# Moving transposed blocks through DRAM: two reads over all 128 partitions in place of four over 32

## The chip, the core and the metric

The kernel runs on one core of a Trainium2 chip. The metric is device time in microseconds (us), the median of several executions of the whole program; less is better. The core has five engines that work side by side: TensorE (PE, matrix products), VectorE (DVE), ScalarE (ACT), GpSimd (POOL) and SyncE (SP). Here SP computes nothing: it issues nearly all DMA transfers, one after another. A DMA is carried out by 16 DMA engines; each of them takes its part of the transfers of one queue in the order in which they were issued.

## What is computed

The input x is 512 tokens of width 1024, in float32. Two layers follow each other, each one normalisation, one input projection, an attention, a gate and an output projection that is added to x:

```
hn   = rms_norm(x, gain)
proj = hn @ w_in                 # queries, keys, values, gate
q, k = rms_norm per head of 64   # 16 heads
out  = softmax(q.k * scale + bias) @ v
x    = x + (out * silu(gate)) @ w_out
```

Layer 0 has three dilation groups (1, 4 and 16) with sliding windows, each with q, k and v of its own, merged by their softmax denominators. Layer 1 is a neighbourhood attention on a grid of 8 x 64 tokens. Products are made from float32 values split into a high and a low part, three matmuls for one product.

## The kernel before

**Tiling.** The 16 heads are worked off in pairs, `hc` = 0 to 7 (`NHC`), 128 columns at a time. For each pair `main_a` (layer 0) or `main_b` (layer 1) projects q, k, v and the gate on PE. In the same stream of PE instructions stands the attention of the pair before, which the generator `side` places between them: PE's order is written out by hand, by a clock in the program (`clock`, `later_on`, `tick`) that counts nominal matmul time. `later_on(delay, job)` issues a DMA when that clock has come far enough; the order of SP's queue follows from it, and SP takes it strictly in order. A DMA that has to wait holds everything behind it on SP.

**Weights.** `raws` (L175) loads blocks of up to 512 KB into three buffers `wraw`. `split` makes the high part `wh` on ACT (L127) and the low part `wl` on POOL or DVE (L131), four buffers each; PE uses them in the projections (`acc`). A load into a `wraw` buffer waits until the block that was there has been split.

**Bias.** `bias_a` loads six small tables for the next pair, `e0` and `e12` (L687 and L692, 704 KB together), from `l_d` in DRAM. The source of each is a pattern of 4 x 32 rows, and its destination has 128 partitions:

```
bass.AP(l0_d.tensor, l0_d.offset + h * 1600 + 127, [[400, 4], [-4, 32], [1, 256]])
```

**The two moves.** A transpose of a 128 x 512 block is made on VectorE in 32 x 32 squares (`nc.vector.transpose`) and completed by a trip through DRAM which takes the squares to other partitions.

- `move_q` (L568) does this for the projected q and k of layer 0, for the pairs 0 and 2 to 5 (`moved`). VectorE transposes the squares of `rawq` (`turn_q`); four writes (L576) put `rawq` into `qd`, write `a` the a-th quarter of every partition's row, 2 KB for each of 128 partitions; four reads (L583) bring `qd` into `qt`. Read `a` fills the 32 partitions from 32a, with four runs of 2 KB each, and needs write `a` alone. From `qt`, `split_q` makes k0h (L602), q0h (L621), k0l and q0l, and with these PE makes the scores (`log`). All four parts must be there.
- `turner` (L713) does it for the softmax probabilities `p`. `put` transposes into `tr` (L724). `send` writes `tr` to `td` (L733) and reads `td` into `pt` (L737), again four and four. In layer 0 each pair from 0 to 6 sends two blocks (u = 0 and 1) of 512 columns a part, in layer 1 each pair from 0 to 5 one of 448. From `pt` PE multiplies the probabilities with v (`o`) during the next pair.

The writes are issued 700 (q) or 1200 to 1500 (p) nominal nanoseconds apart, and the reads 6800 or 9500 to 12000 after the writes. On SP the order in a pair of layer 0 is: four td writes, a weight load, a pt read, six bias loads, a weight load, the remaining pt reads, td writes of the second block with a weight load between, pt reads with weight loads between, four qd writes, a weight load, and the qt reads, also with a weight load between.

Of the kernel before, what the change touches and what calls it, by code (L numbers as in the profile page):

```python
# [13 lines left out]
F32 = mybir.dt.float32  # L14
# [8 lines left out]
P = 128  # L23
# [19 lines left out]
def tile_hybrid_encoder(  # L43
# [13 lines left out]
    nc = tc.nc  # L57
# [8 lines left out]
    dr = ctx.enter_context(tc.tile_pool(name="dr", bufs=1, space=DRAM))  # L66
# [159 lines left out]
    def later_on(delay, job):  # L226

        timers.append((clock[0] + delay, job))
        timers.sort(key=lambda t: t[0])
# [305 lines left out]
    def q_tiles():  # L535


        return (
            wk.tile([P, 512], F32R, tag="q0h", name="q0h", bufs=1),
            wk.tile([P, 512], F32R, tag="q0l", name="q0l", bufs=1),  # L540
            wk.tile([P, 4, 4, P], F32, tag="q12", name="qt", bufs=1),
            wk.tile([P, EXT], F32R, tag="k0h", name="k0h", bufs=1),
            wk.tile([P, EXT], F32R, tag="k0l", name="k0l", bufs=1),
        )

    def q_a(hc):

        yield "wait", ("rawq", hc), 15000 if hc < NHC - 2 else 13000
        raw = st.pop(("rawq", hc))
        if moved(hc):  # L550
            move_q(hc, raw)
            return
        st["q", hc] = q0h, q0l, qt, k0h, k0l = q_tiles()

        tp = transpose4(raw, 0)
        nc.scalar.copy(tjr(q0h), to_tjr(tp))
        nc.vector.tensor_sub(tjr(q0l), to_tjr(tp), tjr(q0h.bitcast(F32)))
        yield
        tp = transpose4(raw, 3 * P)
        put_k([(trj(k0h[:, 64:EXT]), trj(k0l[:, 64:EXT]), to_trj(tp))], 0)  # L560
        yield
        for g in range(2):
            tp = transpose4(raw, (g + 1) * P)
            nc.vector.tensor_copy(qt[:, :, 1 + g, :].rearrange("p t (j r) -> p t j r", j=4), to_tjr(tp))
            yield
        stamp["q", hc] = 0

    def move_q(hc, raw):  # L568

        d = dr.tile([4, P, 512], F32, name="qd", tag="qd", bufs=2)  # L570
        tiles = q_tiles()
        qt, left = tiles[2], [4]

        def write(a):
            src = raw[:, 4 * a : 4 * a + 4].rearrange("p f i r -> p (f i r)")
            tc.keep_in_program_order(nc.sync.dma_start(d[a], src))  # L576
            if a == 3:
                stamp["q", hc] = 0

        def read(a):  # L580
            dst = qt[32 * a : 32 * a + 32].rearrange("k t f x -> k t (f x)")
            src = d[a].rearrange("(t k) x -> k t x", t=4)
            tc.keep_in_program_order(nc.sync.dma_start(dst, src))  # L583
            left[0] -= 1

        for a in range(4):
            later_on(700 * a, partial(write, a))
            later_on(6800 + 700 * a, partial(read, a))

        def land():  # L590
            yield "wait", ("rawq", hc), 27000
            assert not left[0]
            split_q(*tiles)
            st["q", hc] = tiles
            yield

        st["land", hc] = land()

    def split_q(q0h, q0l, qt, k0h, k0l):
        src = qt[:, :, 3, :].rearrange("p t (j r) -> p t r j", j=4)  # L600
        trj4 = lambda t: t[:, 64:EXT].rearrange("p (t r j) -> p t r j", t=4, j=4)
        nc.scalar.copy(trj4(k0h), src)  # L602
        by_t = lambda t: t.rearrange("p (t x) -> p t x", t=4)
        put_k([(by_t(q0h), by_t(q0l), qt[:, :, 0, :])], 0)
        nc.vector.tensor_sub(trj4(k0l), src, trj4(k0h.bitcast(F32)))
# [107 lines left out]
    class turner:  # L713
# [1 line left out]


        def __init__(self, run):
            self.run, self.left = run, 4
            self.t = wk.tile([P, 2048], F32, tag="tr", name="tr", bufs=1)

        def put(self, src, n, off):
# [4 lines left out]
        def send(self, dst, wait, pace):  # L726

            run = self.run
            d = dr.tile([4, P, run], F32, tag="td", name="td", bufs=2)
            place = dst.rearrange("p (a x) -> p a x", a=4)  # L730

            def write(b):
                tc.keep_in_program_order(nc.sync.dma_start(d[b], self.t[:, b * run : b * run + run]))  # L733

            def read(b):
                src = d[b].rearrange("(a k) x -> k a x", a=4)
                tc.keep_in_program_order(nc.sync.dma_start(place[32 * b : 32 * b + 32], src))  # L737
                self.left -= 1

            for b in range(4):  # L740
                later_on(pace * b, partial(write, b))
                later_on(wait + pace * b, partial(read, b))

    def attn_a(hc):
        e0, e12 = st.pop(("e", hc))
# [538 lines left out]
```

## Time and profile before

| | |
|---|---|
| median of 3 executions | 888.09 us (885.46 to 892.52) |
| the profiled execution | 889.36 us |
| its span, first to last instruction | 887.5 us |
| mean granted TensorE clock | 0.983 |
| PE, PE weight load busy | 853.6, 710.0 us |
| DVE, ACT, POOL busy | 513.6, 431.8, 297.8 us |
| moved by DMA | 139.15 MB, mean 157 GB/s |

The page gives busy time by engine, the chain of work that ended last (followed back from the last instruction to what released it) and the DMA issues by size. "A <- B" in the table of waits says that A's engine sat idle until B was done, with the total in us, the count and the longest. In a timeline, a row is start, duration, engine, line, operation, output <- input and count. In a table of windows, the columns are the stretch, its length, busy time (and count) of PE, PE weight load, DVE, ACT and POOL, the granted TensorE clock, the mean busy share of the 16 DMA engines, and GB/s. The chain's rows are start, duration and what ran. SPq is SP's queue: the duration there is that of the issue and not that of the transfer.

### The profile page before, as it was taken

How to read it: one execution, taken by the hardware profiler on the slowest of the kernel's cores; microseconds unless marked ns; L12 is line 12 of the kernel's file. 1: busy time of each engine (PE TensorE's matmuls, PEld its weight loads, DVE VectorE, ACT ScalarE, POOL GpSimd, SP SyncE). 2: the span in 40 equal slices, each digit the busy share in tenths (PEclk: the TensorE clock that was granted, in tenths of full speed). 3: DMA queues.
4: the chain of work that ended last, by engine and by line, in shares of the span. 5: the costliest groups of instructions: out<-in, count | busy, mean ns of one | idle time of the engine just before them, and what ended most of it. 6: DMA issues, size and time to landing. Idle time of an engine off the chain costs nothing.

```text
span 887.5 us, 15473 instructions
## 1 busy us (share of the span) xinstructions
PE 853.6 (96%) x5563; PEld 710.0 (80%) x5563; DVE 513.6 (58%) x1333; ACT 431.8 (49%) x924; POOL 297.8 (34%) x493
## 2 busy tenths in 40 slices
PE   9999999997999799699799999999999999999998
PEld 7787778785788588578678788788989988889786
DVE  7363585672664566367267584537565666666743
ACT  7533565432552552354264454446465556665541
POOL 2342431441442342144143144111433445433411
PEclk9999999999899899799899999999999999999999
DMA  6356366568359268448738366146226556466323
GB/s 240 111 152 193 119 178 169 174 198 198 108 164 256 84 173 245 83 140 229 186 116 220 102 179 182 56 157 200 96 89 167 164 154 174 136 166 185 101 94 129
DMA packets 65469, 139.15 MB, mean 157 GB/s; under 512 B 7024, under 2 KB 24368, under 8 KB 65392
## 3 DMA queue, kind: packets, MB, share of 16 engines
q1 hardware_dynamic: 65104, 138.15, 54.7%
q8 instruction: 44, 0.72, 0.4%
q14 instruction: 33, 0.27, 0.1%
q10 hardware_dynamic: 288, 0.01, 0.0%
HBM read 108.06 MB, written 30.07 MB: 156 GB/s over the span
## 4 chain that ended last, share of the span: by engine, by line
PE 86%; DMA 6%; ACT 3%; DVE 2%; POOL 1%; issue 1%; SPq 1%; ACTq 0%; POOLq 0%; DVEq 0%
PE acc L206 72%; DMA qt<-qd 5%; PE log L206 5%; PE o L206 5%; PE tp L210 3%; ACT wh L127 1%; POOL wl L131 1%; DMA pt<-td 1%; ACT p L1073 1%; ACT k0h L602 0%; DMA hg<-in_head_gain 0%; ACT rawk L458 0%; DVE hn_l L378 0%; DVE q0l L623 0%; ACT p L652 0%
## 5 line engine op out<-in xcount | busy, mean ns | idle before, releaser
L127 ACT CAST wh<-wraw 128x512 fp32r<-128x512 f32 (+1 forms) x276 | 161.7, 587 | 290.4 <-PE acc L206 251.1
L206 PE MATMUL acc<-wh,hn_h 128*128 128x512 f32 (+1 forms) x768 | 294.7, 384 | 1.7 <-ACT rawk L458 1.1
L206 PE MATMUL acc<-wl,hn_h 128*128 128x512 f32 (+1 forms) x768 | 286.1, 373 | 0.7 <-DVE wl L131 0.7
L206 PE MATMUL acc<-wh,hn_l 128*128 128x512 f32 (+1 forms) x768 | 286.1, 373 | 0.0
L131 POOL TENSOR_TENSOR wl<-wraw,wh 128x512 fp32r<-128x512 f32 (+1 forms) x110 | 137.7, 1251 | 367.6 <-ACT wh L127 317.2
L131 DVE TENSOR_TENSOR wl<-wraw,wh 128x512 fp32r<-128x512 f32 (+1 forms) x166 | 112.6, 678 | 140.4 <-ACT wh L127 133.6
L206 PEld LDWEIGHTS acc<-wh,hn_h 128*128 128x128 f32 x768 | 144.9, 189 | 30.0 <-issue 4.3
L206 PEld LDWEIGHTS acc<-wh,hn_l 128*128 128x128 f32 x768 | 144.6, 188 | 20.7
L206 PEld LDWEIGHTS acc<-wl,hn_h 128*128 128x128 f32 x768 | 145.0, 189 | 20.0 <-DVE wl L131 1.0
L206 PE MATMUL acc<-hn_h,wh 128*128 128x512 f32 x192 | 77.0, 401 | 0.3
L272 POOL TENSOR_TENSOR sq<-rawk 128x256 f32<-128x256 f32 x64 | 40.8, 643 | 106.9 <-ACT rawk L458 95.3
L206 PE MATMUL acc<-hn_h,wl 128*128 128x512 f32 x192 | 74.9, 390 | 0.0
L206 PE MATMUL acc<-hn_l,wh 128*128 128x512 f32 x192 | 74.9, 390 | 0.0
L812 ACT ACTIVATE p<-p,mn 128x512 f32<-128x512 f32 (+1 forms) x64 | 44.9, 702 | 57.0 <-DVE mn L801 57.0
L652 ACT ACTIVATE p<-p,mn 128x512 f32<-128x512 f32 (+3 forms) x128 | 69.3, 587 | 0.7 <-DVE mn L651 0.7
L273 DVE TENSOR_REDUCE ss<-sq 128x4 f32<-128x256 f32 (+1 forms) x96 | 48.3, 503 | 26.7 <-POOL sq L272 17.5
L724 DVE STREAM_TRANSPOSE tr<-p 128x512 f32<-128x512 f32 (+1 forms) x80 | 54.0, 685 | 8.4 <-ACT p L652 7.5
L206 PE MATMUL acc<-y_h,wh 128*128 128x512 f32 x128 | 52.1, 407 | 0.0
L206 PE MATMUL acc<-y_h,wl 128*128 128x512 f32 x128 | 50.0, 391 | 0.0
L206 PE MATMUL acc<-y_l,wh 128*128 128x512 f32 x128 | 49.9, 390 | 0.0
L206 PEld LDWEIGHTS acc<-hn_h,wh 128*128 128x128 f32 x192 | 36.1, 188 | 9.8 <-ACT rawk L458 2.1
L206 PEld LDWEIGHTS acc<-hn_h,wl 128*128 128x128 f32 x192 | 36.0, 188 | 7.7
(138 smaller groups left out, 1086.8 us busy)
## 6 DMA issues: line engine op xcount, KB each, us to landing
wraw<-in_w SPq DMA_DIRECT2D x95, 512.0 KB
wraw<-in_w SPq DMA_DIRECT2D x38, 384.0 KB
td<-tr SPq DMA_DIRECT2D x56, 256.0 KB
pt<-td SPq DMA_DIRECT2D x56, 256.0 KB
td<-tr SPq DMA_DIRECT2D x24, 224.0 KB
pt<-td SPq DMA_DIRECT2D x24, 224.0 KB
qd<-rawq SPq DMA_DIRECT2D x20, 256.0 KB
qt<-qd SPq DMA_DIRECT2D x20, 256.0 KB
```

Source lines behind the costliest of these rows:

```text
L127: nc.scalar.copy(h, raw)
L131: eng.tensor_sub(l, raw, h.bitcast(F32))
L206: nc.tensor.matmul(o, l, r, **kw)
L210: nc.tensor.transpose(o, i, ident)
L272: nc.gpsimd.tensor_mul(sq, v, v)
L273: nc.vector.tensor_reduce(ss[:, i * ns : (i + 1) * ns], sq.rearrange("p (a b) -> p a b", b=64), axis=AX.X, op=ALU.add)
L652: nc.scalar.activation(pr, pr, AF.Copy, scale=mn[:, 3:4])
L724: nc.vector.transpose(dst, src[:, :n].rearrange("p (i b k) -> p i b k", b=4, k=32))
L812: nc.scalar.activation(row, row, AF.Exp, bias=mn[:, 1:2], scale=-1.0, accum_out=mn[:, 2:3])
L1073: nc.scalar.activation(pr[:, o : o + n], pr[:, o : o + n], AF.Exp, bias=mn[:, 0:1], scale=-1.0, accum_out=mn[:, 2:3])
```

## The change

In DRAM, `qd` and `td` are laid out with the partition first: `[128, 4, 512]` (or `[128, 4, 448]`) in place of `[4, 128, 512]`. Read `t` (t = 0 and 2) now takes parts t and t + 1 for all 128 partitions, so that a run has 4 KB (3.5 KB in layer 1) on both sides. Two reads take the place of four. The writes keep their number, their source and their 2 KB runs, but write `a` now goes to the rows 32a to 32a + 31 of `d`, viewed part first: a destination of 4 x 32 runs. Every read holds rows of all four writes. The second read is issued 1400 (q), 2400 or 3000 (p) nominal nanoseconds after the first.

```diff
     def move_q(hc, raw):
 
-        d = dr.tile([4, P, 512], F32, name="qd", tag="qd", bufs=2)
+        d = dr.tile([P, 4, 512], F32, name="qd", tag="qd", bufs=2)
         tiles = q_tiles()
-        qt, left = tiles[2], [4]
+        qt, left = tiles[2].rearrange("p t f x -> p t (f x)"), [2]
 
         def write(a):
             src = raw[:, 4 * a : 4 * a + 4].rearrange("p f i r -> p (f i r)")
-            tc.keep_in_program_order(nc.sync.dma_start(d[a], src))
+            dst = d[32 * a : 32 * a + 32].rearrange("k t x -> t k x")
+            tc.keep_in_program_order(nc.sync.dma_start(dst, src))
...
-        def read(a):
-            dst = qt[32 * a : 32 * a + 32].rearrange("k t f x -> k t (f x)")
-            src = d[a].rearrange("(t k) x -> k t x", t=4)
-            tc.keep_in_program_order(nc.sync.dma_start(dst, src))
+        def read(t):
+            tc.keep_in_program_order(nc.sync.dma_start(qt[:, t : t + 2], d[:, t : t + 2]))
             left[0] -= 1
 
         for a in range(4):
             later_on(700 * a, partial(write, a))
-            later_on(6800 + 700 * a, partial(read, a))
+        for t in (0, 2):
+            later_on(6800 + 700 * t, partial(read, t))
...
         def send(self, dst, wait, pace):
 
             run = self.run
-            d = dr.tile([4, P, run], F32, tag="td", name="td", bufs=2)
+            d = dr.tile([P, 4, run], F32, tag="td", name="td", bufs=2)
             place = dst.rearrange("p (a x) -> p a x", a=4)
 
             def write(b):
-                tc.keep_in_program_order(nc.sync.dma_start(d[b], self.t[:, b * run : b * run + run]))
-
-            def read(b):
-                src = d[b].rearrange("(a k) x -> k a x", a=4)
-                tc.keep_in_program_order(nc.sync.dma_start(place[32 * b : 32 * b + 32], src))
+                src, rows = self.t[:, b * run : b * run + run], d[32 * b : 32 * b + 32]
+                tc.keep_in_program_order(nc.sync.dma_start(rows.rearrange("k a x -> a k x"), src))
+
+            def read(a):
+                tc.keep_in_program_order(nc.sync.dma_start(place[:, a : a + 2], d[:, a : a + 2]))
                 self.left -= 1
 
             for b in range(4):
                 later_on(pace * b, partial(write, b))
-                later_on(wait + pace * b, partial(read, b))
+            for a in (0, 2):
+                later_on(wait + pace * a, partial(read, a))
```

More of the change, by code (lines that the diff above doesn't have):

```diff
@@ L717, in __init__ @@
         def __init__(self, run):
-            self.run, self.left = run, 4
+            self.run, self.left = run, 2
             self.t = wk.tile([P, 2048], F32, tag="tr", name="tr", bufs=1)
```

## The prediction

> **What bounds the kernel now.** I read the page first, then the table of waits, then the timeline of the DMA queue in one head group of the first layer, then single windows of the trace for the rate of each kind of transfer.
>
> ```profile
> span 887.5 us, 15473 instructions
> ...
> q1 hardware_dynamic: 65104, 138.15, 54.7%
> ...
> PE 86%; DMA 6%; ACT 3%; DVE 2%; POOL 1%; issue 1%; SPq 1%; ACTq 0%; POOLq 0%; DVEq 0%
> ```
>
> ```profile
> td<-tr SPq DMA_DIRECT2D x56, 256.0 KB
> pt<-td SPq DMA_DIRECT2D x56, 256.0 KB
> td<-tr SPq DMA_DIRECT2D x24, 224.0 KB
> pt<-td SPq DMA_DIRECT2D x24, 224.0 KB
> qd<-rawq SPq DMA_DIRECT2D x20, 256.0 KB
> qt<-qd SPq DMA_DIRECT2D x20, 256.0 KB
> e<-l_d SPq DMA_DIRECT2D x32, 112.0 KB
> e<-l_d SPq DMA_DIRECT2D x16, 128.0 KB
> ```
>
> TensorE bounds it: 86% of the chain that ended last is PE. Beside it stands a DMA share of 6%. The blocks that the change touches are 20 moves of td to pt and 5 of qd to qt, each four writes and four reads. All of them share one queue (SP's) with the weight loads.
>
> ```profile
> PE log L206 <- ACT q0h L621: 24.3, 4, 7.6
> ...
> ACT wh L127 <- PE acc L206: 251.1, 156, 4.4
> ACT k0h L602 <- DMA qt<-qd: 31.2, 5, 8.6
> ACT wh L127 <- DMA wraw<-in_w: 26.5, 11, 4.4
> ```
>
> This says where the DMA stands on the path. PE stops four times, 24.3 us in all, for q0h, which is made from qt: in hc 2 to 5 the move of q lands after PE has come to the scores. (The fifth moved group, hc 0, costs PE nothing.) Weights are different: ACT's splits wait 251.1 us for PE to free a buffer and only 26.5 us for a weight load. So later weights have cover; a later qt has none.
>
> **The change, step by step.** First the order of the work. In the built program PE, DVE, ACT and POOL keep their order but for a split or two and a memset that change places. On SP, 50 reads disappear (80 pt to 40, 20 qt to 10). At about 0.4 us of SP time each this is nothing, as SP mostly waits. Three things change in the transfers.
>
> (a) The reads: 128 partitions of 4 KB runs in place of 32 partitions. (b) The writes: same bytes, same 2 KB runs, but the built destination is now 4 x 32 x 512 where it was 128 x 512, its outermost count being 4. (c) The first read now spans rows of all four writes, so it waits for the last of them; read a waited for write a only.
>
> ```profile
> 237.00:239.50 2.50, 2.50 (x13) 1.94 (x11) 0.69 (x1) 0.62 (x1) 2.34 (x5) 1.00 0.88 332
> 247.00:251.00 4.00, 4.00 (x21) 3.32 (x20) 3.55 (x8) 2.96 (x6) 0.30 (x2) 1.00 0.24 56
> 246.00:252.00 6.00, 6.00 (x32) 4.99 (x31) 4.94 (x9) 4.58 (x9) 0.73 (x3) 1.00 0.28 76
> 115.60:119.10 3.50, 2.39 (x65) 1.97 (x45) 3.50 (x15) 1.52 (x4) 2.35 (x4) 1.00 1.08 221
> 591.00:594.00 3.00, 3.00 (x15) 2.49 (x14) 1.18 (x3) 1.09 (x3) 0.00 (x0) 1.00 0.92 348
> ```
>
> The last two columns are the busy share of the 16 DMA engines and GB/s. First row: old td writes, 332 GB/s at 0.88, so 377 GB/s with all engines busy, or 23.6 for each. Fourth row: old reads into 32 partitions, 221 GB/s with every engine busy. Fifth row: full-width loads of 4 KB runs, 348 at 0.92, so 378. Half a MB (0.524 MB) read full-width thus takes 1.4 us, a whole block 2.8 in place of 4.7: (a) saves 1.9 us a block.
>
> The second row decides (b). In it only the six bias loads e<-l_d of a group are in flight, and 0.24 of the engines are busy: 4 of 16. Their source pattern (line 687) has outermost count 4, with 128 partitions on the other side, the mirror image of the new writes. So I expect the new writes on 4 engines. At 23.6 GB/s each (same 2 KB runs, so the nearest row) that is 94 GB/s: one write 2.8 us, a block 11.1 us in place of 2.8, or 8.3 us more. At the rate of the bias loads, 56 GB/s, a block would take 18.7 us: that is the other end.
>
> [...]
>
> Now one group, hc 3, whose queue reads:
>
> ```profile
> 235.32 2.13 SPq L733 DMA_DIRECT2D td<-tr  x4
> ...
> 243.97 1.11 SPq L687 DMA_DIRECT2D e<-l_d  x2
> 245.12 3.19 SPq L692 DMA_DIRECT2D e<-l_d  x4
> ...
> 253.01 0.34 SPq L733 DMA_DIRECT2D td<-tr  x1
> ...
> 257.90 2.76 SPq L733 DMA_DIRECT2D td<-tr  x3
> 265.86 1.92 SPq L737 DMA_DIRECT2D pt<-td  x2
> 267.88 0.85 SPq L175 DMA_DIRECT2D wraw<-in_w  x2
> ...
> 273.59 2.10 SPq L576 DMA_DIRECT2D qd<-rawq  x4
> ...
> 280.13 0.90 SPq L583 DMA_DIRECT2D qt<-qd  x2
> ...
> 281.96 0.90 SPq L583 DMA_DIRECT2D qt<-qd  x2
> ```
>
> ```profile
> 292.00 1.08 ACT k0h L602
> ...
> 294.88 3.11 PE log L206 x70
> ```
>
> I follow the four busy engines, which take their transfers in the order of issue. Terms: half-MB load or read 1.4; new write 2.8; the bias burst (0.721 MB at 56 to 76 GB/s) 9.5 to 12.9, so 11.2; 2 us from issue to moving (td issued at 235.32 moves at 237).
>
> - td writes of the first half: 237.0 + 4 x 2.8 = 248.2. A weight load: 249.6.
> - The pt read waits on SP until 248.2 and holds the bias loads behind it (before: issued at 243.97). It moves from 250.5 to 251.9; the bias burst ends at 263.1.
> - Weight load 264.5, second pt read 265.9, one td write 268.7, weight load 270.1, three td writes 278.5.
> - SP stands at the next pt read until 278.5 (before: 265.86); behind it stand three weight loads and the qd writes. pt, two weight loads, pt, weight load, moving from 280.6: 287.6.
> - qd writes: 287.6 + 11.2 = 298.8. The first qt read is issued at 299, moves from 301; qt, weight load, qt: 305.2.
>
> Before, qt was there at 292.0 (k0h starts). So 13.2 us later, and PE waits for it already: the whole 13.2 goes on the path. Weight loads held up by 12 us, with splits that run ahead of PE (the 251.1 us above), may starve PE before the scores, but that stall lies inside the longer wait for q and is not added.
>
> Groups hc 3, 4 and 5 have this order in the built program: 3 x 13.2 = 39.6. In hc 2 the burst starts at once and q comes later after it:
>
> ```profile
> 170.25 1.10 SPq L687 DMA_DIRECT2D e<-l_d  x2
> ...
> 180.49 1.44 SPq L733 DMA_DIRECT2D td<-tr  x3
> ...
> 201.38 1.96 SPq L576 DMA_DIRECT2D qd<-rawq  x4
> ```
>
> ```profile
> 219.68 1.07 ACT k0h L602
> ```
>
> The same sum: burst 172.3 to 183.5, weight, td, weight 189.1, three td 197.5, pt from 199.5, then as above 206.5, qd 217.7, qt from 219.9 to 224.1: 4.4 us late. Elsewhere (hc 0, 1, 6) qd or td writes are 8.3 us longer without a wait of PE now; bounds 0 and 20, I take 4.5, as the ACT rows above show cover.
>
> In the second layer the cover is larger:
>
> ```profile
> 218.00:291.00 73.00, 66.72 (x452) 53.87 (x452) 39.75 (x100) 32.19 (x62) 23.18 (x36) 0.95 0.61 169
> ...
> 645.00:860.00 215.00, 214.02 (x1367) 188.28 (x1366) 137.54 (x419) 124.85 (x334) 86.33 (x163) 1.00 0.52 146
> ```
>
> PE is busy 214.02 of 215 us, and a 224 KB block (9.7 us in place of 2.4) comes once in six groups, each with a whole group before its use. I cost it at 0; if the cover were gone, 6 x 7.3 = 44 us is the most. The granted clock is 0.95 in the stage of hc 3 where it is 1.00 without stalls: each stall is followed by slower matmuls already, so a longer one adds 0 to 2 us; I take 0.
>
> Sum: 39.6 + 4.4 + 4.5 = 48.5. The profiled execution took 889.36 us (span 887.5), the median is 888.09. 889.4 + 48.5 = 938.
>
> **Rivals.**
> 1. Faster: the writes still use 16 engines, since 128 partitions stand on their other side. Then only (a) and (c) act. The second qt read, issued at 281.96 in hc 3 behind a weight load that waits for its buffer, finds the queue nearly empty and lands near 286, 6 us sooner; the 24.3 us of waits go, and part of the 0.05 x 73 us of clock in four stages, 14 us: 24 to 38, say 29: 860. For it: nothing in this trace has the count of 4 on the destination. Against: the 0.24. It decides if a write takes under some 5 us a block. [...]
> 2. Saturated: the four engines move writes at 56 GB/s. Three blocks of 18.7, a burst of 11.2, ten weight loads and six reads at 1.4 are 90 us in a group of 73: the four engines bound the first layer. Each block adds 7.6 us to the sum above, twice to three times a group: some 95 us over it, 1035. Against: 2 KB aligned runs moved at 23.6 an engine.
> 3. Drained: the queue empties between td and qd, and only qd's own block counts, 8.3 - 1.9 = 6.4 in four groups: 915. Against: SP's wait at 265.86 directly ahead of qd.
> 4. Hidden, within 1% (in which a measurement can't tell a change of this kernel from none): it would need q's wait to absorb the 8.3, but PE has no slack there.
>
> **How the numbers follow.** My forecast 0.72, drained 0.08, faster 0.09, saturated 0.08, hidden 0.03. The time is 938, the forecast's. Its own bounds: the burst at 9.5 or 12.9 is 1.7 us either way in four groups (7), the other groups 0 or 20 in place of 4.5, the clock 8 more: 926 to 969. Downwards the drained case (915) is taken in, upwards some way to the saturated one: 905 to 990. Left out are faster, saturated and hidden, 0.20 together. Faster 0.09, same 0.03, slower 0.88.
>
> **What would show it.** In the changed profile: windows with td writes alone at a DMA share near 0.25 and under 100 GB/s (b); reads at 350 GB/s or more (a); pt reads on SP waiting for td writes by 5 to 12 us in each group (c); PE log waiting for q0h about 70 us in place of 24.3. A td write window at 0.8 or more, or qt landing sooner, makes the forecast wrong; waits of PE for weights in the second layer make it too low.

## The result and the profile after

The changed kernel takes 954.6 us (median of 4 executions, 950.54 to 955.85), the kernel before 890.31 us on the same chip (4 executions, 885.46 to 893.94). The ratio is 1.0718, with a 95% interval of 1.0652 to 1.0784: slower by 64 us. The forecast was 938 us, in a range of 905 to 990.

The page of the changed kernel: its span, the row of SP's DMA queue (packets, MB, share of the 16 engines' time), and the chain that ended last.

```profile
span 952.4 us, 15406 instructions
...
q1 hardware_dynamic: 56704, 138.14, 43.1%
...
PE 60%; DMA 23%; SPq 5%; DVE 5%; ACT 4%; issue 2%; POOL 1%; ACTq 0%; DVEq 0%
PE acc L206 49%; DMA qd<-rawq 8%; DMA td<-tr 7%; PE log L206 4%; PE o L206 4%; DMA qt<-qd 3%; DMA wraw<-in_w 3%; PE tp L210 3%; SPq L577 1%; SPq L734 1%; SPq L692 1%; DMA e<-l_d 1%; SPq L175 1%; DVE wl L131 1%; ACT rawq L458 1%
```

The same bytes are moved in fewer packets, and the DMA engines' time for them even falls, from 54.7% to 43.1%. Yet DMA rises from 6% to 23% of the chain, and its two largest parts are the writes, `qd` 8% and `td` 7%. The engines do less and are waited for more.

The waits, of all engines (A <- B: total us, count, longest):

```profile
ACT wh L127 <- PE acc L206: 198.8, 131, 4.4
...
ACT wh L127 <- DMA wraw<-in_w: 101.9, 17, 12.6
...
ACT k0h L602 <- DMA qt<-qd: 61.3, 5, 13.5
...
PE log L206 <- ACT q0h L621: 43.8, 4, 12.4
...
PE acc L206 <- ACT wh L127: 9.9, 5, 3.5
...
PE acc L206 <- ACT rawk L458: 7.3, 1, 7.3
...
PE acc L206 <- POOL wl L131: 5.1, 5, 1.7
```

and of SP's queue, first after, then before:

```profile
SPq L737 <- DMA td<-tr: 152.2, 32, 11.3
...
SPq L582 <- DMA qd<-rawq: 43.7, 10, 8.0
```

```profile
SPq L737 <- DMA td<-tr: 25.4, 11, 6.9
...
SPq L583 <- DMA qd<-rawq: 10.3, 7, 3.7
```

PE waits 43.8 us for q0h where it waited 24.3, ACT 101.9 us for weights where it waited 26.5, and SP stands 195.9 us behind the writes where it stood 35.7. The rate of the transfers is in the windows (last columns: granted clock, busy share of the 16 DMA engines, GB/s). Only td writes are in flight in the first, only reads and a weight load in the second:

```profile
290.00:296.00 6.00, 4.53 (x23) 3.42 (x21) 6.00 (x9) 1.62 (x3) 1.67 (x1) 1.00 0.26 102
```

```profile
321.50:325.00 3.50, 0.00 (x0) 0.00 (x0) 0.00 (x0) 0.00 (x0) 0.00 (x0) 0.50 1.00 350
```

Writes run at 102 GB/s on a quarter of the engines (10.3 us for a block of 1.049 MB; they ran at 332), reads at 350 (they ran at 221). Both halves of the change are visible, and the bad half is larger. The clock of 0.50 in the second row belongs to PE, which has nothing to do there.

Where the time went, by pair. Each stretch ends with the first matmul of the pair's scores (`log`). The windows of after for the stretches of hc 0 to 3 (length, then busy time of PE, PE weight load, DVE, ACT, POOL):

```profile
0.00:97.30 97.30, 87.68 (x382) 70.03 (x382) 48.56 (x93) 44.33 (x83) 29.64 (x45) 0.97 0.46 154
97.30:150.80 53.50, 52.40 (x372) 42.86 (x371) 34.51 (x95) 26.09 (x51) 17.56 (x32) 0.96 0.46 155
150.80:240.90 90.10, 75.49 (x494) 60.41 (x493) 40.68 (x100) 33.91 (x66) 26.93 (x41) 0.95 0.49 169
240.90:327.30 86.40, 70.17 (x452) 55.54 (x452) 40.72 (x101) 31.83 (x63) 23.86 (x36) 0.90 0.43 143
```

In hc 3 PE is idle for 16.2 of 86.4 us, and its granted clock is 0.90. The length of every stretch in us, the forecast beside it, and two experiments told of below (only the move of q changed, only that of p changed):

| stretch to the scores of | before | after | added | forecast | q alone, added | p alone, added |
|---|---|---|---|---|---|---|
| hc 0 | 90.4 | 97.3 | 6.9 | in 4.5 | 5.6 | 2.4 |
| hc 1 | 51.7 | 53.5 | 1.8 | in 4.5 | 2.2 | 2.2 |
| hc 2 | 79.4 | 90.1 | 10.7 | 4.4 | 2.9 | 7.8 |
| hc 3 | 72.3 | 86.4 | 14.1 | 13.2 | 3.3 | 10.5 |
| hc 4 | 74.2 | 85.9 | 11.7 | 13.2 | 1.8 | 10.3 |
| hc 5 | 71.9 | 86.2 | 14.3 | 13.2 | 3.6 | 10.9 |
| hc 6 | 60.6 | 64.7 | 4.2 | in 4.5 | 0.8 | 2.8 |
| hc 7 | 55.3 | 55.3 | 0.0 | 0 | 0.0 | 0.0 |
| rest (layer 2) | 331.9 | 333.0 | 1.2 | 0 | 0.4 | 1.0 |
| span | 887.5 | 952.4 | 64.9 | 48.5 | 20.5 | 47.8 |

### The profile page after: what moved, and what is told of

It is laid out like the page before. It is cut to its first block, busy times and chain, and to the rows that moved or that the text cites. A ratio compares the mean times of both kernels' runs of the same rounds, so it can differ in the third digit from the quotient of the medians.

```text
span 952.4 us, 15406 instructions
## 1 busy us (share of the span) xinstructions
PE 870.8 (91%) x5563; PEld 718.7 (75%) x5563; DVE 515.2 (54%) x1333; ACT 429.6 (45%) x924; POOL 300.0 (32%) x493
## 3 DMA queue, kind: packets, MB, share of 16 engines
q1 hardware_dynamic: 56704, 138.14, 43.1%
## 4 chain that ended last, share of the span: by engine, by line
PE 60%; DMA 23%; SPq 5%; DVE 5%; ACT 4%; issue 2%; POOL 1%; ACTq 0%; DVEq 0%
PE acc L206 49%; DMA qd<-rawq 8%; DMA td<-tr 7%; PE log L206 4%; PE o L206 4%; DMA qt<-qd 3%; DMA wraw<-in_w 3%; PE tp L210 3%; SPq L577 1%; SPq L734 1%; SPq L692 1%; DMA e<-l_d 1%; SPq L175 1%; DVE wl L131 1%; ACT rawq L458 1%
## 5 line engine op out<-in xcount | busy, mean ns | idle before, releaser
L206 PE MATMUL acc<-wh,hn_h 128*128 128x512 f32 (+1 forms) x768 | 300.8, 392 | 23.8 <-ACT wh L127 9.9
L206 PE MATMUL acc<-wl,hn_h 128*128 128x512 f32 (+1 forms) x768 | 291.1, 379 | 5.9 <-POOL wl L131 5.1
L206 PE MATMUL acc<-wh,hn_l 128*128 128x512 f32 (+1 forms) x768 | 290.6, 378 | 0.0
L131 POOL TENSOR_TENSOR wl<-wraw,wh 128x512 fp32r<-128x512 f32 (+1 forms) x110 | 140.6, 1278 | 382.3 <-ACT wh L127 357.5
L206 PEld LDWEIGHTS acc<-wh,hn_h 128*128 128x128 f32 x768 | 147.5, 192 | 56.4 <-ACT wh L127 12.7
L206 PEld LDWEIGHTS acc<-wl,hn_h 128*128 128x128 f32 x768 | 148.0, 193 | 27.3 <-POOL wl L131 6.8
L206 PEld LDWEIGHTS acc<-wh,hn_l 128*128 128x128 f32 x768 | 147.2, 192 | 22.0
L724 DVE STREAM_TRANSPOSE tr<-p 128x512 f32<-128x512 f32 (+1 forms) x80 | 53.5, 683 | 19.5 <-DMA td<-tr 14.6
L206 PE MATMUL log<-k0h,q0h 64*128 64x192 f32 (+1 forms) x64 | 12.0, 373 | 43.8 <-ACT q0h L621 43.8
L605 DVE TENSOR_TENSOR k0l<-qt,k0h 128x512 fp32r<-128x512 f32 x5 | 5.3, 1067 | 77.7 <-ACT k0h L602 77.7
```

Source lines behind the costliest of these rows:

```text
L131: eng.tensor_sub(l, raw, h.bitcast(F32))
L206: nc.tensor.matmul(o, l, r, **kw)
L724: nc.vector.transpose(dst, src[:, :n].rearrange("p (i b k) -> p i b k", b=4, k=32))
```

## The experiments

Theory A is the prediction's: the writes to a destination of 4 x 32 runs use 4 of the 16 DMA engines, and the late q is what PE pays. Where the expectations set others against it, S blames SP, which stands still until all four writes have landed, and P holds that the number of partitions which a read fills is what decides. Theories B, C and D are told where they are used.

**Only the writes slow.** Reads and waits are as before. The DRAM buffer keeps its order but is padded to 33 rows for each group of 32, so that the destination of a write can't be joined into 128 rows; the reads skip the padding.

```diff
-        d = dr.tile([4, P, 512], F32, name="qd", tag="qd", bufs=2)
+        d = dr.tile([4, 4, 33, 512], F32, name="qd", tag="qd", bufs=2)
...
-            tc.keep_in_program_order(nc.sync.dma_start(d[a], src))
+            tc.keep_in_program_order(nc.sync.dma_start(d[a, :, 0:32], src))
```

(and the same for `td`).

> The kernel before, with its four reads into 32 partitions, but qd and td padded in DRAM so that a write has the destination 4 x 32 x 512. Only the writes change. Theory A: writes at 4 engines, 11 us a block; q lands 8 us or more later in each moved group; the old reads add 1.9 us a block to what the changed kernel has: 945 to 980. Theory B: the time of the kernel before, 880 to 895.

958.43 us, ratio 1.0784 (1.0726 to 1.0843). A window with td writes in flight, a wait of PE, and a wait of SP:

```profile
287.00:291.00 4.00, 1.21 (x6) 0.71 (x5) 3.76 (x11) 1.62 (x3) 1.17 (x1) 1.00 0.25 98
```

```profile
PE log L206 <- ACT q0h L621: 52.6, 4, 13.9
```

```profile
SPq L737 <- DMA td<-tr: 77.0, 37, 6.9
```

The writes run at 98 GB/s on a quarter of the engines, and the shape of the destination alone does the whole damage. SP's hold for td is half of that in the changed kernel (77.0 against 152.2 us) and the time is the same within the intervals: theory S falls as the cause. The run also says that wide reads and the joint wait, taken together, are worth about nothing once the writes are slow. That the writes and the bias loads stand in the queue of the same four engines is seen in hc 3 of this kernel:

```profile
262.44 1.68 SPq L687 DMA_DIRECT2D e<-l_d  x2
```

```profile
264.00:274.00 10.00, 10.00 (x49) 8.30 (x48) 5.22 (x10) 6.58 (x14) 2.63 (x5) 1.00 0.27 94
```

Bias loads are issued while td writes are still under way (issued from 253.81 on, some 10 us of moving), and yet the share stays at a quarter until both are done; on engines of their own the two, at a quarter each, would add up to about half.

**The same layout with writes on all engines.** Write `a` takes the a-th quarter of the partitions with its whole row, so that both sides have 32 outermost. A read of parts t and t + 1 then needs only writes t and t + 1. (For `td` the same.)

```diff
-            src = raw[:, 4 * a : 4 * a + 4].rearrange("p f i r -> p (f i r)")
-            dst = d[32 * a : 32 * a + 32].rearrange("k t x -> t k x")
+            src = raw[32 * a : 32 * a + 32].rearrange("k (b f) i r -> k b (f i r)", b=4)
+            dst = d[:, a].rearrange("(b k) x -> k b x", b=4)
```

> Reads as in the changed kernel. Each write now takes 32 partitions of the source with all four parts (destination and source 32 x 4 x 512, outermost count 32); read t needs writes t and t + 1 only. Theory A (the writes run on 4 engines because the outermost count of the destination is 4): the writes spread over 16 engines again, a block of writes takes 3 to 5 us in place of 11, windows of td writes show a DMA share over 0.7, PE waits for q0h at most 24 us, time 865 to 895. Theory B (the loss comes from the wider reads and their waits, not from the count of engines): time stays above 930.

865.35 us, ratio 0.9739 (0.9687 to 0.9792): faster than before. A window with writes alone, and PE's wait:

```profile
232.50:234.50 2.00, 2.00 (x11) 1.64 (x9) 0.69 (x1) 0.62 (x1) 1.76 (x5) 1.00 0.94 243
```

```profile
PE log L206 <- ACT q0h L621: 5.5, 4, 1.6
```

The reads are those of the changed kernel, the buffer's layout too. Only how a write is cut differs, and with it which writes a read waits for (the single read below separates the two), and the time falls from 954.6 to 865.35 us. A block is written in 4.3 us (1.049 MB at 243 GB/s) in place of 10.3.

**One half of the change alone.** First the move of q changed and that of p as before, then the reverse.

> The change in the move of q only, the move of p as before. Theory A by the sum on record: in hc 2 to 5 the queue is empty when qd's writes start, so q lands 8.3 - 1.9 = 6.4 us later, hc 0 loses some 6 us more: 889 + 26 + 6 + clock = 915 to 930. Theory C (nearly all of the loss is in the move of q): 945 to 955. Theory D (nearly all in the move of p, whose writes stand ahead of q): 890 to 900.

910.67 us, ratio 1.0246 (1.0182 to 1.031): slower, and just under what was expected.

> The change in the move of p only, the move of q as before. Theory A by the sum on record: the four engines are free 8 us later when qd's writes start, in hc 3 to 5, less in hc 2: q lands 6 to 8 us later in three groups: 889 + 22 + clock = 910 to 925. Theory C: 888 to 900. Theory D: 945 to 955.

937.6 us, ratio 1.0523 (1.0446 to 1.06), above what was expected. The halves add up: 20.5 + 47.8 = 68.3 us of span against 64.9. They don't divide as the forecast's ledger would have it, though. In hc 3 to 5, p alone adds 31.7 us and q alone 8.6. SP's queue of p alone shows why:

```profile
247.62 2.90 SPq L734 DMA_DIRECT2D td<-tr  x4
...
290.57 0.34 SPq L737 DMA_DIRECT2D pt<-td  x1
291.01 0.85 SPq L175 DMA_DIRECT2D wraw<-in_w  x2
291.91 0.42 SPq L737 DMA_DIRECT2D pt<-td  x1
292.43 0.60 SPq L175 DMA_DIRECT2D wraw<-in_w  x1
293.09 2.88 SPq L576 DMA_DIRECT2D qd<-rawq  x4
```

```profile
314.80 1.07 ACT k0h L602
```

From the first td write to the first qd write are 45.5 us, 7.2 more than before (235.32 to 273.59 is 38.3). But from there to k0h are 21.7 us too, where 18.4 were before (273.59 to 292.00), although this half of the code is the old one. The wait at 290.57 has gathered two reads and three weight loads into 2.5 us directly ahead of the q writes; before, four reads and three weight loads were issued over 5.8 us (265.86 to 271.61). So slow td writes cost q twice: by the wait on SP (7.2 us) and in q's own leg (3.3 us), there probably by the traffic which that wait bunches.

**The bias loads from 128 rows.** In the changed kernel the six tables are filled from x, with 128 rows outermost (below, one of `e0`; those of `e12` likewise). The bias is thereby left out of the result.

```diff
-                bass.AP(l0_d.tensor, l0_d.offset + h * 1600 + 127, [[400, 4], [-4, 32], [1, 256]]),
+                xt[:, h % KT, 0:256],
```

> The changed kernel, but the six bias loads of a pair in layer 0 take the same number of bytes from x, with 128 rows outermost on both sides, so that they run on 16 engines; the bias tables are left out (filled with x), so the output is another. Theory A (what counts is the queue of the same four engines, which the burst shares with the writes): the burst leaves them, some 9 us a pair, so q lands 7 to 10 us sooner in hc 2 to 5: 915 to 930. Theory S (what counts is SP, which stands at the reads until all four writes have landed; the burst does not matter): 945 to 957.

928.31 us, ratio 1.0417 (1.0382 to 1.0452). The time is where theory A put it, 26 us below the changed kernel. The stretches of hc 2 to 5 are 4.5 to 6.1 us shorter, where q was expected 7 to 10 sooner. No window shows the share of these loads themselves; that they left the four engines is an inference from the td writes of the kernel before, which have 128 rows outermost on both sides too and showed 0.88. How much of the 26 us is the sharing of four engines with the new writes isn't shown: the kernel before has the same bias loads, and it was not run without them. SP's hold for td (146.8 us) is nearly that of the changed kernel, so it isn't what went away. ACT's waits for weights fall back, and q stays late:

```profile
ACT wh L127 <- DMA wraw<-in_w: 31.7, 8, 8.4
```

```profile
PE log L206 <- ACT q0h L621: 49.2, 4, 14.6
```

**What the width of the reads is worth.** Both kernels have the good writes of the second experiment and reads that wait for all four of them: one has a single read over 128 partitions with runs of 8 KB, the other four reads of 32 partitions each, with the same runs. The cuts show the move of q; that of p is changed alike.

```diff
-            tc.keep_in_program_order(nc.sync.dma_start(qt[:, t : t + 2], d[:, t : t + 2]))
+            tc.keep_in_program_order(nc.sync.dma_start(qt[:, 0:4], d[:, 0:4]))
```

> The version with writes by quarter of the partitions (865.35), but one read of all four parts over 128 partitions (1 MB, runs of 8 KB) in place of two; it waits for all four writes. If the joint wait costs by itself, q lands later than with two reads, 870 to 880; if only the count of engines of the writes matters, 862 to 870.

861.34 us, ratio 0.9672 (0.964 to 0.9703): the best of all, though its interval overlaps that of the two reads. This read waits for all four writes, as the first read of the changed kernel does, so the joint wait isn't what made that kernel slow.

```diff
-            tc.keep_in_program_order(nc.sync.dma_start(qt[:, t : t + 2], d[:, t : t + 2]))
+            tc.keep_in_program_order(nc.sync.dma_start(qt[32 * t : 32 * t + 32], d[32 * t : 32 * t + 32]))
```

> The version with writes by quarter, but four reads into 32 partitions each (runs of 8 KB), each waiting for all four writes. Against one_read only the width of the read differs. If the width is what gains (1.9 us a block by the rates on record), q lands 2 to 4 us later in hc 2 to 5 and the waits of PE come back: 872 to 885. If the width does not matter: within 3 us of one_read.

889.99 us, ratio 1.0008 (0.9981 to 1.0035), above what was expected. PE waits again as in the kernel before:

```profile
PE log L206 <- ACT q0h L621: 20.8, 4, 6.0
```

The gap of 28.7 us between the two is what one wide read is worth here against four narrow ones, and it is more than I had given it. It isn't the width alone, as the expectation has it: the four reads are also issued one after another. In hc 3 the last of them is issued 2.8 us later after the first qd write than the single read (9.4 against 6.6), and k0h follows 4.9 us later (17.2 against 12.3). Against the kernel before, writes by quarters with narrow reads bring nothing; the gain over it comes with the wide reads.

**Wide reads from the old layout.** The writes and the DRAM buffer are those of the kernel before; read `a` fetches part a for all 128 partitions in runs of 2 KB, so that now its source is the pattern of 4 x 32 rows. Each read now needs all four writes. (For `td` the same.)

```diff
-            dst = qt[32 * a : 32 * a + 32].rearrange("k t f x -> k t (f x)")
-            src = d[a].rearrange("(t k) x -> k t x", t=4)
+            dst = qt[:, a].rearrange("p f x -> p (f x)")
+            src = bass.AP(d.tensor, d.offset + 16384 * a, [[65536, 4], [512, 32], [1, 512]])
```

> The kernel before with its layout in DRAM and its writes (128 x 512, 16 engines), but each of the four reads now fills one part of all 128 partitions, 2 KB a run; the source of such a read is 4 x 32 runs, so the outermost count of 4 has moved from the write to the read. Theory A (the smaller outermost count of the two sides sets the engines, whichever side it stands on): reads on 4 engines, 11 us a block, windows with reads alone at a DMA share near 0.25 and under 100 GB/s, PE waits for q0h over 45 us; 930 to 970. Theory P (128 partitions on the SBUF side suffice for a fast read): 855 to 870.

987.4 us, ratio 1.113 (1.1069 to 1.119): the slowest kernel of all, beyond theory A's figures, and far from those of P.

```profile
334.00:338.00 4.00, 0.00 (x0) 0.00 (x0) 0.00 (x0) 0.00 (x0) 0.00 (x0) 0.50 0.26 100
```

```profile
PE log L206 <- ACT q0h L621: 65.5, 4, 16.7
```

In this window only qt reads are in flight; they fill 128 partitions and still run at 100 GB/s on a quarter of the engines. So in these kernels the count of 4 did the same on either side (0.26 and 100 GB/s here, 0.25 and 98 with the slow writes), and 128 partitions on the other side didn't help. Slow reads cost 29 us more than slow writes alone (958.43), and the queue of hc 3 shows in which leg: from the first td write to the first qd write are 39.9 us (43.1 with slow writes, 38.3 before), and from there to k0h 35.5 (27.5 and 18.4). The slow pt reads are issued directly ahead of the qd writes, and the slow qt reads follow them; that both stand in q's own leg is the likely reason, which no run separates.

## Why the prediction came out as it did

**The mechanism was right.** The writes take a quarter of the engines (0.26, 102 GB/s, where 0.24 and 94 were expected), and that the shape of their destination is the cause is shown by the padded kernel (slow with nothing else changed) and by the writes by quarters (fast with the reads of the changed kernel, and with the single read that waits for all four writes). The reads run at 350 GB/s, as expected.

**The ledger of hc 3 to 5 was right, in its parts too.** SP's queue of after in hc 3:

```profile
255.13 2.94 SPq L734 DMA_DIRECT2D td<-tr  x4
...
278.71 4.39 SPq L734 DMA_DIRECT2D td<-tr  x3
...
297.58 0.33 SPq L737 DMA_DIRECT2D pt<-td  x1
...
300.07 7.33 SPq L577 DMA_DIRECT2D qd<-rawq  x4
```

```profile
325.58 1.08 ACT k0h L602
```

From the first td write to the pt read that lets SP go on (297.58): 42.5 us, where the ledger had 43.2 (278.5 less 235.32) and the kernel before 30.5. From there to k0h: 28.0, where the ledger had 26.7 (305.2 less 278.5) and the kernel before 26.1. Together that is 13.8 more than before, where the ledger said 13.2; the three stretches became 40.1 us longer, where it said 39.6. What each write does alone (10.6 for p, 2.9 for q in a stretch) is another matter: an added delay of one leg also changes what is queued before the next, so shares read off a ledger of the whole aren't what an edit of one leg brings.

**One sign came out otherwise.** PE's wait for q0h was to be about 70 us and is 43.8, though hc 3 to 5 grew as forecast. PE itself comes to the scores later. Of the 64.9 us of span, 19.5 are longer waits for q0h; 28.2 are other idle time, above all the weights (`wh` 9.9, `wl` 5.1), whose stalls the prediction had set inside the wait for q, and `rawk` in hc 0 (7.3); and 17.2 are longer busy time, at a granted clock of 0.956 in place of 0.983. So the wait for q0h isn't the price of a late q. With the bias loads from 128 rows it is longer (49.2), in a kernel that is 26 us faster.

**Hc 2 was too small, 4.4 against 10.7.** The step that failed is the words "the burst starts at once". SP's queue there, before and then after:

```profile
159.12 0.80 SPq L737 DMA_DIRECT2D pt<-td  x2
```

```profile
161.47 3.72 SPq L734 DMA_DIRECT2D td<-tr  x3
...
176.35 0.33 SPq L737 DMA_DIRECT2D pt<-td  x1
176.77 1.15 SPq L409 DMA_DIRECT2D rp<-in_rpb  x1
...
184.39 1.14 SPq L687 DMA_DIRECT2D e<-l_d  x2
```

Ahead of the burst stands a pt read, and ahead of that the td writes of the block before. SP now stands there until 176.35, and a one-time chain of small tables (from `rp` on) and the bias loads follow behind it. Counted from the start of the pair's stretch, the bias loads are issued at 33.6 us in place of 28.2 (184.39 less 150.8; 170.25 less 142.0): 5.4 late. From there to k0h (239.15 in the chain of waits) the delay is 5.3 us, close to the 4.4 of the ledger. I began the ledger at a transfer without asking what SP stands at before it.

**Hc 0, 1 and 6 were given too little, 4.5 against 12.9 together** (within the bounds of 0 to 20). Half of it is hc 0, which the prediction held to be covered since its q cost PE nothing. The chain of waits of after shows the way, from the qd writes to the scores:

```profile
72.38 13.56 DMA qd<-rawq
...
86.42 5.22 DMA qt<-qd
...
91.71 0.09 ACT k0h L602
...
93.40 1.55 ACT wh L127 x3
94.95 0.74 ACT rawk L458 x2
...
95.74 1.65 PE acc L206 x3
```

PE stops 7.3 us, and not for q0h. ACT waits 13.5 us for qt to make k0h (2.9 before), and behind k0h on ACT, at 93.40 and 94.95, come the weight splits and the `rawk` eviction for which PE waits. Having written that a wait costs what is queued behind it, I asked this of SP and not of ACT. The other half is hc 1 with 1.8, which is the clock's (below), and hc 6 with 4.2, of which 2.6 are a wait of PE for `vt` and most of the rest is longer busy time.

**The clock.** The term of 0 (0 to 2 for each stall) was nearly right for the sum and wrong as a picture. PE's busy time rises by 17.2 us (853.6 to 870.8), which is more than those stalls were given. In hc 3 to 5 this lies inside the wait for q, since the stretches grew by the ledger's amount. It shows as time in hc 1, where PE idles 1.1 us before and after, but is busy for 52.40 in place of 50.49 us, at a granted clock of 0.96 in place of 1.00. After the stall of hc 3:

```profile
327.50:331.00 3.50, 3.37 (x68) 2.72 (x76) 2.44 (x5) 1.01 (x3) 0.65 (x1) 0.50 0.02 5
331.00:335.00 4.00, 4.00 (x35) 2.97 (x20) 3.44 (x20) 3.11 (x9) 0.61 (x1) 0.68 0.00 0
335.00:339.00 4.00, 4.00 (x51) 2.84 (x49) 2.49 (x7) 4.00 (x10) 1.36 (x3) 1.00 0.00 0
```

The matmuls restart at a clock of 0.50 and are at 1.00 by 335. A mean of 0.68 over the four us between puts the change at 333.6 us, some 6.2 us after the restart (331.0 to 333.5 shows 0.50, and 333.6 to 335.0 shows 1.00). What makes the clock fall, and what makes it rise just there, no run shows.

**The rivals.** Rival 1 (the writes keep all engines, 860 us) didn't happen, but it named the right price for the wrong kernel: it is what the writes by quarters give, 865.35, and the single read, 861.34. Saturated is out, as the writes ran at 102 GB/s and not at 56; so is hidden, as the time rose by 64 us; so is drained, as hc 3 grew by 14.1 us and not by 6.4, and SP's wait until 297.58 stands directly ahead of qd.

**Layer 2** was costed at 0 and grew by 1.2 us.

## What to carry to other kernels

A new DRAM layout has two ends: when it makes one side of a transfer wide, write down the built pattern of the other side and look at its outermost count, since here a count of 4 on either side left a quarter of the engines (shares of 0.24 to 0.26) and turned a gain of 25 us into a loss of 64. The cut matters, not the layout: with writes by 32 partitions, so that 32 stands outermost on both sides, the same buffer and the same reads gave 865 us against 890. And when a transfer becomes late, go through every in-order queue that waits for it (SP, and the engine which evicts for PE), as well as the engine that reads it.

## What the runs showed of the hardware

A window of the kernel before in which only reads into 32 partitions are in flight:

```profile
115.60:118.00 2.40, 1.29 (x61) 1.06 (x41) 2.40 (x12) 0.61 (x1) 2.35 (x4) 1.00 1.07 214
```

- Transfers of 32 partitions ran at 214 GB/s into SBUF (this window; the one up to 119.1 with 221 has the start of a weight load in it) and at 243 out of it (the writes by quarters, share 0.94). With 128 partitions reads and a weight load ran at 350 (the changed kernel) and writes at 332 (the kernel before, share 0.88). So with 32 partitions the reads came to 0.61 of the rate with 128, the writes to 0.73; why the two differ, no run shows.
- A busy share near 1 isn't full speed: the narrow reads of the kernel before show 1.07 at 214 GB/s, the wide ones 1.00 at 350, and the changed kernel's engines are busy for less (43.1% against 54.7%) while it is slower. The share adds up the time that packets took; it doesn't say what they move.
- The trace also has the times at which the parts of a transfer landed (on its semaphore). In the kernel before, a td write lands in 16 parts (the one issued at 235.32: from 237.24 to 237.90) and the last bias load, issued at 247.18, in four from 257.48 to 259.05, after a single signal at 248.72. In the changed kernel a td write has four as well (the one issued at 255.13: from 260.57 to 261.32, after a single signal at 256.07). This agrees with the shares of a quarter.
- The order shows there too. The kernel before issues a weight load at 249.77, behind the six bias loads. Twelve of its 16 parts land by 255.35 and the last four from 258.91 to 260.33, behind the four of the last bias load (257.48 to 259.05); ACT, which waits for it, goes on at 260.43. The four transfers issued next land their last parts in the order of issue, at 260.99, 261.91, 262.60 and 263.12.
